# A hybrid attention trunk on one core: five buffers for the first modulation rows, two K tiles ahead of the weights, and c loaded as one row

## The chip, the core and the metric

The kernel runs on one core of a Trainium2 chip. A core has a matrix engine (TensorE: PE for its matmuls, PEld for its weight loads), three engines for elementwise work (VectorE: DVE, ScalarE: ACT, GpSimd: POOL), an engine that here only issues transfers (SyncE: SP), and 16 DMA engines that carry what SP's and ACT's queues hand them. Matmuls read SBUF and accumulate in PSUM banks. The metric is device microseconds (us) of one launch; lower is better.

## What is computed

A streaming encoder of two layers, batch 1, 256 tokens, model width 2048, all in float32. A conditioning vector `c` of 2048 numbers gives each layer six modulation vectors of 2048 (shift, scale and gate for the mixer, the same for the FFN):

```python
c_act = jax.nn.silu(c)
for i in range(DEPTH):
    mod = c_act @ ada_w[i] + ada_b[i]
    sh1, sc1, g1, sh2, sc2, g2 = [m[:, None, :] for m in jnp.split(mod, 6, axis=-1)]
    h = rms_norm(x, norm_mix_g[i]) * (1.0 + sc1) + sh1
    y = even_mixer(h, ...) if i % 2 == 0 else odd_mixer(h, ...)
    x = x + g1 * y
    h = rms_norm(x, norm_ffn_g[i]) * (1.0 + sc2) + sh2
    x = x + g2 * conv_ffn(h, ...)
return rms_norm(x, final_g)
```

The even mixer (layer 0) projects `h` once by `ev_w_in` (2048 columns in, 3400 out) to the queries, keys and values of sliding-window attention and of a sparse latent attention with an index; the odd mixer is stick-breaking attention. The FFN is gated with a short convolution over tokens, 5632 wide.

## The kernel before, in words

Activations lie feature-major: 16 K tiles (`DB`) of 128 features by 256 tokens. `xT` is the input in that form, loaded in four transfers. The kernel is written with a tile framework: pools hand out named tiles with a number of buffers for each tag, a new tile of a tag waits until the one whose buffer it takes has been read for the last time, and a scheduler places the instructions on each engine. Each engine, and SP's queue of transfers, then runs its list strictly in order.

**Weights.** All weight matrices stream through in pieces of 128 x 1024 (512 KiB). `make_piece` (L145 on) takes a tile `w` of tag `ring` (6 buffers) and has SP load it. Pieces of the first projection (`w_ev`) are multiplied as they are, in float32. For all later pieces ScalarE writes a rounded copy `hi` (L159) and VectorE the rest `lo` (L161), each in three buffers of a pool `split`, and TensorE runs three matmuls for one: hi x hi, hi x lo, lo x hi (`dense`, `pair_steps` L213 to L215, `token_steps`). `units` makes one piece ahead (`AHEAD`) of the one in use.

**Modulation.** The modulation is done as 192 jobs (`JOBS`), in the order in which they are used: scale and shift row of K tile 0, of K tile 1, and so on. `ada_step` (L107 on) takes a tile of tag `ada` (two buffers of 128 x 2048, 1 MiB), has SP load the job's weights (L118), and VectorE multiplies them by `c_act`, which holds silu(c) in every partition, and sums along the row (L120). For a scale row a short instruction (L124) makes the factor `a`. `ada_until` runs jobs up to the one that is needed; `beat`, called with each weight piece, spreads the later ones over the time.

**The opening** (`even_mixer`, L425 on). The sum of squares of `xT` is formed by ScalarE (L416) and VectorE (L420) in tiles `sq_in` of the pool `split`, TensorE sums over partitions (`nps_in`), GpSimd takes the power, and `r_in` is the reciprocal norm. Then a loop over the 16 K tiles: `modulate` runs the tile's two modulation jobs, VectorE writes `xn_m` = r x a x xT (L319), ScalarE adds the shift and writes `hT_m` (L321), and TensorE multiplies that tile into eight open PSUM accumulators (`c_lat`, `va` L221 and six `pair` L228: 16 matmuls, a step here), which takes two weight pieces. After the loop come the rest of the projections and the attention (`q` L234 is the first matmul there).

**The start.** SP loads `c_act` (c already repeated for 128 partitions, 1 MiB), then `xT`, then the early parameters `par`; ScalarE's queue loads small constants (`con` among them). ScalarE applies silu to all of `c_act` (L103).

## Time and profile before

| | |
|---|---|
| Time, median of 3 runs | 2358.72 us (2341.0 to 2361.32) |
| The profiled execution: time, span | 2362.08 us, 2360.3 us |
| TensorE matmuls busy | 2283.0 us (97% of the span) |
| VectorE, ScalarE, GpSimd busy | 1738.4, 1092.9, 12.0 us |
| Mean granted clock of TensorE | 0.99 |
| Moved by DMA | 606.03 MB, mean 257 GB/s |
| `ada` loads | 192 of 1024 KB |
| Weight loads `w` | 528 + 96 + 64 + 58 of 512 KB |

The span runs from the first to the last instruction of one profiled execution. A busy matmul engine is not an engine at its peak, since matmuls are pipelined and their ends are modelled. In a timeline a row gives the start, the time from the first instruction of the row to the end of its last, engine, source line, operation, what it writes and reads, and in brackets how long the engine was idle before and what ended that. The chain of waits goes back from the last instruction of a stretch to what released it each time. The granted clock is given as a share of TensorE's 2.4 GHz.

### The profile page before, as it was taken

The numbers are of one execution on the slowest core, as the hardware profiler recorded it, in microseconds if no ns is written. First come the engines' busy times: TensorE is split into PE (matmuls) and PEld (weight loads), VectorE is DVE, ScalarE is ACT, GpSimd is POOL, SyncE is SP. The second block draws the span as 40 slices with busy tenths as digits, with TensorE's granted clock in tenths as the row PEclk, the third lists the DMA queues.
The fourth block names the chain that finished last, engine by engine and source line by source line (L and its number), as shares of the span: only waits on it lengthen the run. The fifth ranks groups of instructions, "written<-read, shape, count | busy, mean of one in ns | idle before, by whom it ended". The sixth has DMA issues, their size and how long they took to land.

```text
span 2360.3 us, 44197 instructions
## 1 busy us (share of the span) xinstructions
PE 2283.0 (97%) x18340; PEld 2240.1 (95%) x18340; DVE 1738.4 (74%) x2390; ACT 1092.9 (46%) x1553; POOL 12.0 (1%) x26
## 2 busy tenths in 40 slices
PE   5889999899999999999999999999999999999998
PEld 4768899899999999999999999999999999999998
DVE  4557689998887888888887676878766656656655
ACT  1013354455553554454456655645555445445434
POOL 1000000000000000000000000000000000000000
PEclk9999999999999999999999999999999999999999
DMA  8998988788888888888867777676766666666663
GB/s 313 344 335 326 331 305 312 286 313 302 303 298 299 304 300 304 300 304 301 304 226 240 237 238 239 226 260 204 231 188 187 187 186 185 188 187 187 188 187 118
DMA packets 141929, 606.03 MB, mean 257 GB/s; under 512 B 15584, under 2 KB 20256, under 8 KB 117024
## 3 DMA queue, kind: packets, MB, share of 16 engines
q1 hardware_dynamic: 136656, 597.67, 74.8%
q10 hardware_dynamic: 5072, 5.54, 0.8%
q8 instruction: 143, 2.34, 0.4%
q14 instruction: 58, 0.48, 0.1%
HBM read 601.00 MB, written 2.15 MB: 256 GB/s over the span
## 4 chain that ended last, share of the span: by engine, by line
PE 53%; issue 32%; DMA 7%; DVE 6%; ACT 1%; POOL 0%; ACTq 0%; DVEq 0%; POOLq 0%; SPq 0%
PE up L215 7%; PE up L213 7%; PE up L214 7%; DMA ada<-in_w_ada_dram 6%; DVE ada L120 4%; PE dn L213 3%; PE dn L214 3%; PE dn L215 3%; PE o L213 2%; PE o L215 2%; PE o L214 2%; PE cq L213 1%; PE ck L213 1%; PE cq L214 1%; PE ck L214 1%
## 5 line engine op out<-in xcount | busy, mean ns | idle before, releaser
L159 ACT ACTIVATE hi<-w 128x1024 fp32r<-128x1024 f32 x688 | 728.6, 1059 | 890.7 <-PE up L214 389.6
L161 DVE TENSOR_TENSOR lo<-w,hi 128x1024 fp32r<-128x1024 f32 x688 | 840.5, 1223 | 402.5 <-ACT hi L159 399.9
L213 PE MATMUL up<-hT_f,hi 128*128 128x256 f32 x2816 | 789.5, 281 | 2.8 <-ACT hT_f L323 2.2
L215 PE MATMUL up<-hT_f,lo 128*128 128x256 f32 x2816 | 788.6, 280 | 0.2 <-DVE lo L161 0.2
L214 PE MATMUL up<-hT_f,hi 128*128 128x256 f32 x2816 | 787.4, 280 | 0.0
L213 PEld LDWEIGHTS up<-hT_f,hi 128*128 128x128 f32 x2816 | 529.5, 188 | 3.7 <-ACT hT_f L323 2.9
L215 PEld LDWEIGHTS up<-hT_f,lo 128*128 128x128 f32 x2816 | 530.6, 189 | 0.5 <-DVE lo L161 0.4
L214 PEld LDWEIGHTS up<-hT_f,hi 128*128 128x128 f32 x2816 | 529.9, 188 | 0.0
L120 DVE CUSTOM_DVE_ANT_0 ada<-ada,c_act,par 128x2048 f32<-128x2048 f32 x192 | 450.5, 2346 | 78.8 <-DMA ada<-in_w_ada_dram 78.7
L214 PE MATMUL dn<-gT,hi 128*128 128x256 f32 x1364 | 383.8, 281 | 0.0
L215 PE MATMUL dn<-gT,lo 128*128 128x256 f32 x1364 | 383.8, 281 | 0.0
L213 PE MATMUL dn<-gT,hi 128*128 128x256 f32 x1364 | 383.8, 281 | 0.0
L215 PEld LDWEIGHTS dn<-gT,lo 128*128 128x128 f32 x1364 | 262.1, 192 | 0.0
L213 PEld LDWEIGHTS dn<-gT,hi 128*128 128x128 f32 x1364 | 256.1, 188 | 0.0
L214 PEld LDWEIGHTS dn<-gT,hi 128*128 128x128 f32 x1364 | 256.1, 188 | 0.0
L228 PE MATMUL pair<-hT_m,w 128*128 128x256 f32 x384 | 89.1, 390 | 0.0
L228 PEld LDWEIGHTS pair<-hT_m,w 128*128 128x128 f32 x384 | 76.6, 199 | 11.6
L349 DVE SCALAR_TENSOR_TENSOR xT<-dn,mod,xT 128x256 f32<-128x256 f32 x128 | 56.4, 478 | 25.4 <-PE dn L215 20.2
L228 PE MATMUL q<-hT_m,w 128*128 128x256 f32 x320 | 73.7, 382 | 0.0
L213 PE MATMUL cq<-hT_m,hi 128*128 128x256 f32 x256 | 72.2, 282 | 1.1 <-ACT hT_m L323 1.1
L214 PE MATMUL cq<-hT_m,hi 128*128 128x256 f32 x256 | 72.1, 282 | 0.0
L213 PE MATMUL ck<-hT_m,hi 128*128 128x256 f32 x256 | 72.0, 281 | 0.0
(260 smaller groups left out, 3071.3 us busy)
## 6 DMA issues: line engine op xcount, KB each, us to landing
w<-in_w_f_dram SPq DMA_DIRECT2D x528, 512.0 KB, 4.4
ada<-in_w_ada_dram SPq DMA_DIRECT2D x192, 1024.0 KB, 6.5
w<-in_w_od_dram SPq DMA_DIRECT2D x96, 512.0 KB, 4.4
w<-in_w_o_dram SPq DMA_DIRECT2D x64, 512.0 KB, 5.3
w<-in_w_ev_dram SPq DMA_DIRECT2D x58, 512.0 KB, 7.9
bias<-bias_rows ACTq DMA_DIRECT2D x16, 256.0 KB, 6.2
xT<-in_x_dram SPq DMA_DIRECT2D x4, 512.0 KB, 7.6
c_act<-in_c_dram SPq DMA_DIRECT2D x1, 1024.0 KB, 4.9
```

The lines of the kernel that those rows point to most:

```text
L120: nc.vector.tensor_tensor_reduce(w, w, c_act, scale=1.0, scalar=pr("ada_b")[:, s * DB + b:s * DB + b + 1], op0=ALU.mult, op1=ALU.add, accu ...
L159: nc.scalar.activation(hi, raw, AF.Copy)
L161: sub = nc.vector.tensor_tensor(lo, raw, hi.bitcast(F32), op=ALU.subtract)
L213: nc.tensor.matmul(o, hi[:, js], xh, start=k == first and j == 0, stop=False, skip_group_check=True)
L214: nc.tensor.matmul(o, hi[:, js], xl, start=False, stop=False, skip_group_check=True)
L215: nc.tensor.matmul(o, lo[:, js], xh, start=False, stop=k == last, skip_group_check=True)
L228: nc.tensor.matmul(acc[:, j * S:(j + 1) * S], w[:, j * P:(j + 1) * P], xs[:, k], start=k == first and j == 0, stop=k == last, skip_group_c ...
L349: nc.vector.scalar_tensor_tensor(xT[:, b], acc, g, xT[:, b], op0=ALU.mult, op1=ALU.add)
```

## The change

Five things change. `c` is loaded as a single row of 2048 numbers (into a buffer of tag `ada`); four matmuls with a row of ones spread it over 128 partitions into four PSUM banks, and ScalarE applies silu from there, 512 columns at a time. Of the first 32 modulation jobs the odd ones (the shift rows of layer 0's mixer) take their buffer from the pool `split`, whose tiles are now 8 KiB a partition and there are three of them; the even ones (scale rows) keep the two `ada` buffers. For that, `hi` and `lo` of a weight piece become the two halves of one tile `parts`. The `sq_in` tiles move to tiles that the mixer uses later. In the opening the modulation jobs of K tile k + 2 (`LEAD`) are asked for before the work on K tile k.

```diff
--- before.py
+++ after.py
@@ -28,6 +28,7 @@
 PIECE = 8
 RING = 6
 AHEAD = 1
+LEAD = 2
 SH1, SC1, G1, SH2, SC2, G2 = range(6)
 
 JOBS = []
@@ -72,7 +73,8 @@
         return ps.tile([P, 512], F32, tag=tag, bufs=BANKS[tag], name=name)
 
     c_act = keep.tile([P, D], F32, name="c_act")
-    nc.sync.dma_start(c_act, c)
+    c_row = ring.tile([P, D], F32, tag="ada", bufs=2, name="c_row")[:1]
+    nc.sync.dma_start(c_row, c)
     par = keep.tile([P, P_W], F32, name="par")
     rb = keep.tile([32, 32], F32, name="rb")
     nc.scalar.dma_start(rb, rel_bias)
@@ -100,7 +102,12 @@
     nc.vector.memset(mhalf, -0.5)
 
 
-    nc.scalar.activation(c_act, c_act, AF.Silu)
+    one_row = keep.tile([1, P], F32, name="one_row")
+    nc.vector.memset(one_row, 1.0)
+    for i, tag in enumerate(("acc", "acc", "s", "s")):
+        spread = bank(tag, f"c_ps{i}")
+        nc.tensor.matmul(spread, one_row, c_row[:, i * 512:(i + 1) * 512], start=True, stop=True)
+        nc.scalar.activation(c_act[:, i * 512:(i + 1) * 512], spread, AF.Silu)
     mod = keep.tile([P, 12, DB], F32, name="mod")
     scaled = {(l, k): keep.tile([P, DB], F32, name=f"a_{k}{l}") for k in (SC1, SC2) for l in (0, 1)}
     pace = {"rate": 0.0, "due": 0.0, "hold": 0, "behind": False}
@@ -114,7 +121,10 @@
         ada["made"] += 1
         layer, kind, b = JOBS[i]
         s = layer * 6 + kind
-        w = ring.tile([P, D], F32, tag="ada", bufs=2, name=f"ada{i}")
+        if i < 2 * DB and i % 2:
+            w = split.tile([P, D], F32, tag="parts", name=f"ada{i}")
+        else:
+            w = ring.tile([P, D], F32, tag="ada", bufs=2, name=f"ada{i}")
         nc.sync.dma_start(w, w_ada[i])
         end = mod[:, s, b:b + 1]
         nc.vector.tensor_tensor_reduce(w, w, c_act, scale=1.0, scalar=pr("ada_b")[:, s * DB + b:s * DB + b + 1],
@@ -155,9 +165,9 @@
             flow["pieces"][i] = (raw,)
             beat()
             return
-        hi = split.tile([P, n], F32R, tag="hi", name=f"hi{i}")
+        parts = split.tile([P, 2, n], F32R, tag="parts", name=f"parts{i}")
+        hi, lo = parts[:, 0], parts[:, 1]
         nc.scalar.activation(hi, raw, AF.Copy)
-        lo = split.tile([P, n], F32R, tag="lo", name=f"lo{i}")
         sub = nc.vector.tensor_tensor(lo, raw, hi.bitcast(F32), op=ALU.subtract)
         flow["pieces"][i] = (hi, lo)
         if pace["behind"]:
@@ -412,7 +422,7 @@
             hT = keep.tile([P, DB, S], F32, tag="hT", name="hT_m0")
             total = None
             for k in range(0, DB, 4):
-                sq = split.tile([P, 4, S], F32, tag="lo", name=f"sq_in{k}")
+                sq = pool.tile([P, 4, S], F32, tag="oS1" if k == 0 else "oS2" if k % 8 else "qi", bufs=1, name=f"sq_in{k}")
                 nc.scalar.activation(sq, xT[:, k:k + 4], AF.Square)
                 if total is None:
                     total = sq
@@ -424,6 +434,7 @@
             early = [(token_steps32, bank("acc", "c_lat")), (token_steps32, bank("acc", "va"))]
             early += [(pair_steps32, bank(tag, f"pair{i}")) for i, tag in enumerate(("acc", "s", "s", "o", "t", "t"))]
             for k in range(DB):
+                ada_until(0, SH1, min(k + LEAD, DB - 1))
                 modulate(hT, r, 0, SC1, SH1, "m0", [k])
                 for steps_, acc in early:
                     if steps_ is token_steps32:
@@ -866,7 +877,7 @@
     out = {}
     out["x"] = f["x"][0].T.reshape(DB, P, S).transpose(1, 0, 2)
     sink_order = [8 * (g // 2) + 4 * (s // 2) + 2 * (g % 2) + s % 2 for g in range(4) for s in range(4)]
-    out["c"] = broadcast(f["c"])
+    out["c"] = f["c"].reshape(1, D)
     out["params"] = np.concatenate([
         cols(f["ada_b"], 2), cols(f["norm_mix_g"], 2), cols(f["norm_ffn_g"], 2), cols(f["final_g"], 1),
         broadcast(f["ev_sinks"][0][sink_order]), broadcast(f["ev_kv_norm_g"][0]), cols(f["ffn_conv_w"], 6),
```

The scheduler puts this into each engine's list. Below is SP's list of transfers right after `par`, first before the change (`ada_147` and `ada_151` are the scale and the shift row of K tile 0, `ada_179` and `ada_183` those of K tile 1, `w_157` the first weight piece):

```order
L118 DMA ada_147<-in_w_ada_dram 128x2048
L118 DMA ada_151<-in_w_ada_dram 128x2048
L152 DMA w_157<-in_w_ev_dram 128x1024
L152 DMA w_159<-in_w_ev_dram 128x1024
L152 DMA w_169<-in_w_ev_dram 128x1024
L118 DMA ada_179<-in_w_ada_dram 128x2048
L118 DMA ada_183<-in_w_ada_dram 128x2048
L152 DMA w_189<-in_w_ev_dram 128x1024
```

and the same place after the change (`ada_161` and `ada_165` are K tile 0, `ada_168` and `ada_172` K tile 1, `ada_175` and `ada_179` K tile 2, `ada_207` and `ada_211` K tile 3, `w_185` the first weight piece):

```order
L128 DMA ada_161<-in_w_ada_dram 128x2048
L128 DMA ada_165<-in_w_ada_dram 128x2048
L128 DMA ada_168<-in_w_ada_dram 128x2048
L128 DMA ada_172<-in_w_ada_dram 128x2048
L128 DMA ada_175<-in_w_ada_dram 128x2048
L128 DMA ada_179<-in_w_ada_dram 128x2048
L162 DMA w_185<-in_w_ev_dram 128x1024
L162 DMA w_187<-in_w_ev_dram 128x1024
L162 DMA w_197<-in_w_ev_dram 128x1024
L128 DMA ada_207<-in_w_ada_dram 128x2048
L128 DMA ada_211<-in_w_ada_dram 128x2048
L162 DMA w_217<-in_w_ev_dram 128x1024
```

Six modulation rows now stand ahead of the first weight piece, where two stood; from there on it is two rows and two pieces in turn, as before. After the last row six pieces follow where two did.

VectorE's list from the last addition of squares on, before the change (`ISA` with three inputs is a reduction, the `ISA` behind it reads its sum out):

```order
L420 TENSOR_TENSOR sq_in_110<-sq_in_110,sq_in_118 128x1024
L304 TENSOR_SCALAR v_in<-nps_in 128x2
L120 ISA ada_147,mod<-ada_147,c_act,par 128x2048
L120 ISA mod 128x1
L124 SCALAR_TENSOR_TENSOR a_93<-mod,par 128x1
L319 SCALAR_TENSOR_TENSOR xn_m_154<-r_in,a_93,xT 128x256
L120 ISA ada_151,mod<-ada_151,c_act,par 128x2048
```

and after it:

```order
L430 TENSOR_TENSOR sq_in_124<-sq_in_124,sq_in_132 128x1024
L130 ISA ada_161,mod<-ada_161,c_act,par 128x2048
L130 ISA mod 128x1
L314 TENSOR_SCALAR v_in<-nps_in 128x2
L134 SCALAR_TENSOR_TENSOR a_107<-mod,par 128x1
L130 ISA ada_165,mod<-ada_165,c_act,par 128x2048
```

The first reduction now stands ahead of the norm's `v_in`, and the first shift row's reduction ahead of the first `xn_m` (which follows it). Further on the scheduler has also placed some instructions of the mixer and the first FFN a little earlier or later among each other.

## Rows read from the trace of the kernel before

**Rows 1.** Windows: stretch, length; busy us (instructions) by engine; clock; DMA share; GB/s.
```profile
0.00:180.00 180.00, 133.06 (x544) 109.74 (x544) 91.00 (x111) 23.21 (x46) 7.82 (x20) 0.95 0.89 332
600.00:1000.00 400.00, 400.00 (x3398) 400.00 (x3397) 338.37 (x424) 188.32 (x240) 0.00 (x0) 1.00 0.87 302
```

**Rows 2.** Chain of waits, 0 to 200 us: start us, us, what.
```profile
25.29 5.12 DMA ada<-in_w_ada_dram
...
77.68 5.72 DMA ada<-in_w_ada_dram
...
136.55 7.62 DMA ada<-in_w_ada_dram
```

**Rows 3.** Waits, 0 to 180 us: us in total, times, longest us.
```profile
DVE ada L120 <- DMA ada<-in_w_ada_dram: 58.9, 17, 5.0
```

**Rows 4.** The waits of SP's own queue, 0 to 180 us, same columns.
```profile
SPq L118 <- DVE a L124: 76.7, 15, 9.6
```

**Rows 5.** Timeline, one round of the opening: start us, us, what [idle before <-releaser].
```profile
136.55 3.38 SPq L118 DMA_DIRECT2D ada<-in_w_ada_dram  x2
...
140.03 1.11 SPq L152 DMA_DIRECT2D w<-in_w_ev_dram  x2
...
140.18 1.13 PE L221 MATMUL c_lat<-w,hT_m 128*128 128x256 f32 x4 [2.92 <-ACT hT_m L321]
...
146.59 3.38 SPq L118 DMA_DIRECT2D ada<-in_w_ada_dram  x2
```

**Rows 6.** Timeline, TensorE: first, second and last step's start, next stage's first matmul.
```profile
30.36 2.08 PE L221 MATMUL c_lat<-w,hT_m 128*128 128x256 f32 x4 [3.81 <-ACT hT_m L321]
...
39.85 1.03 PE L221 MATMUL c_lat<-w,hT_m 128*128 128x256 f32 x4
...
170.63 1.13 PE L221 MATMUL c_lat<-w,hT_m 128*128 128x256 f32 x4 [1.15 <-ACT hT_m L321]
...
177.64 1.46 PE L234 MATMUL q<-hT_m,w 128*128 128x256 f32 x6
```

**Rows 7.** Windows: four stretches of the opening, columns as in rows 1.
```profile
8.00:20.00 12.00, 1.24 (x5) 0.78 (x4) 4.44 (x6) 7.09 (x6) 0.00 (x0) 1.00 1.02 417
60.00:90.00 30.00, 26.78 (x121) 22.32 (x120) 19.86 (x24) 2.03 (x4) 0.00 (x0) 1.00 0.99 376
90.00:160.00 70.00, 54.73 (x223) 45.04 (x221) 36.90 (x42) 3.05 (x6) 0.00 (x0) 0.93 0.87 310
166.00:180.00 14.00, 12.82 (x61) 10.64 (x59) 5.73 (x12) 8.12 (x24) 0.73 (x1) 1.00 1.02 408
```

**Rows 8.** Timeline of the first 28 us: what stands ahead of the first reduction.
```profile
7.01 1.46 PE L398 MATMUL vb_ps<-oh,rb 32*32 32x384 f32 x2 [7.01 <-DMA oh<-in_onehot_dram]
...
11.44 1.91 ACT L103 ACTIVATE c_act<-c_act 128x2048 f32<-128x2048 f32 x1
...
13.26 2.93 ACT L416 ACTIVATE sq_in<-xT 128x1024 f32<-128x1024 f32 x3
...
16.61 2.56 DVE L420 TENSOR_TENSOR sq_in<-sq_in,sq_in 128x1024 f32<-128x1024 f32 x2
...
22.91 2.34 DVE L120 CUSTOM_DVE_ANT_0 ada<-ada,c_act,par 128x2048 f32<-128x2048 f32 x1
...
27.01 0.48 DVE L319 SCALAR_TENSOR_TENSOR xn_m<-r_in,a,xT 128x256 f32<-128x256 f32 x1 [1.55 <-ACT r_in L423]
```

**Rows 9.** Waits from 180 us to the end: us in total, times, longest us.
```profile
ACT hi L159 <- PE up L214: 389.6, 284, 3.2
...
PE up L215 <- DVE lo L161: 0.2, 1, 0.2
```

**Rows 10.** Timeline in the first FFN: one weight piece split, and the next.
```profile
699.69 1.06 ACT L159 ACTIVATE hi<-w 128x1024 fp32r<-128x1024 f32 x1 [1.17 <-PE up L214]
...
700.78 1.23 DVE L161 TENSOR_TENSOR lo<-w,hi 128x1024 fp32r<-128x1024 f32 x1 [1.24 <-ACT hi L159]
...
702.52 1.06 ACT L159 ACTIVATE hi<-w 128x1024 fp32r<-128x1024 f32 x1 [1.32 <-issue]
```

## The prediction

> **What bounds the kernel now.** I read the busy times by stage first. TensorE is busy without a gap in a stretch of 400 us in the middle, but only 133.1 of the first 180 us [rows 1]. So time can be won at the front and nowhere near as easily behind it: what the opening loses, the rest, which is TensorE after TensorE, carries to the end unchanged. That is why I add what happens before 180 us to the end of the program one to one.
>
> Next comes the chain of waits inside the opening. It is one pattern, repeated for each of the 15 K tiles after the first: a load of a modulation row (`ada`) lands, VectorE reduces it in 2.35 us, the next load is issued, and that takes 5 to 8 us to land. The first such load takes 5.12 us (with no other transfer under way), one at 77.68 takes 5.72 us, one at 136.55 takes 7.62 us [rows 2]. VectorE stands idle for these loads 58.9 us in 17 waits [rows 3], and SP, which issues them, is itself blocked 76.7 us on the same reductions [rows 4]. One round is in [rows 5]: SP issues at 136.55 and next at 146.59, 10.04 us later; in between TensorE starts its step 2.92 us late. The cause is that the scale rows share two buffers with the shift rows: a load can't be issued before the row two places ahead of it is consumed. It is latency in a loop, not work: VectorE's own work per tile is two reductions of 2.35 us and three short instructions.
>
> What would the step cost otherwise? TensorE's 16 matmuls of a step take 7.01 us (from the last step's start, 170.63, to the first matmul of the next stage, 177.64), and 9.49 us in the first step, 30.36 to 39.85, which begins slower [rows 6]. A step's transfers are two `ada` rows of 1 MiB and two weight pieces of 0.5 MiB, 3.146 MB. In the two stretches in which requests are queued without a break, 8 to 20 and 166 to 180 us, the rate is 417 and 408 GB/s; in the opening's loop it is 376 (60 to 90 us) and then 310 (90 to 160 us) [rows 7]. At 408 GB/s a MiB takes 2.57 us and a step 7.71 us. So the transfers, no longer the loop, would set the pace, TensorE 10% behind them.
>
> **The change part by part.** *Buffers.* Scale rows now have the two `ada` buffers to themselves and shift rows three others. Before a scale row is issued, the row of two K tiles earlier must be reduced, no longer that of the tile just before. Between landing and use there are then some 5 MiB queued, 13 us at 408 GB/s, against 2.35 us for a reduction and at most another 3 us of VectorE's queue ahead of it. The loop's wait is covered, with room. The weight ring (6 pieces) asks that TensorE be done three steps back, which it is as long as TensorE is less than two steps late. So I take the steady pace from the transfers.
>
> *The start.* This part can lose. The first weights now stand behind six modulation rows in SP's queue, not two, and the third scale row (`ada_175`) waits for the reduction of the first. That reduction needs all of `c_act` and stands behind VectorE's last addition of squares, which ends at 16.61 + 2.56 = 19.17 [rows 8]. The reduction takes 2.34 us, and before the change SP issued its next load 0.04 us after it, at 25.29 [rows 2, 8]: 21.6 here. A lone load of 5.12 us [rows 2] then lands at 26.7; the shift row behind it 2.57 us; the first weight piece 1.29 us: 30.6. TensorE's first step began at 30.36 [rows 6], so the start is about where it was. The modulated tile is there by then: the first normalised tile starts at 27.01 [rows 8], and its shift row has already been reduced.
>
> *c as one row.* It takes 1 MiB off the queue (2.57 us at 408 GB/s) and lets the con and x tiles land sooner. Against that stand four matmuls of 512 columns and four activations in place of one of 1.91 us. A matmul of this kind is the first of the trace, 384 columns in 1.46 us, right after a long idle time [rows 8]; for 512 columns that is 1.95 us, four make 7.8 us after 8.47, so 16.3, and the last quarter of the activation (0.5 us) 16.8 where it ended at 13.35: 3.4 us late at worst, with the squares behind it. At best everything is 2.57 us earlier. The two are near each other in size, matmuls that follow each other get faster, so I take nothing, and keep -2.6 and +3.4 us for the range; both go to the end one to one, since the third scale row hangs on them.
>
> *hi and lo in one tile.* After the opening ScalarE may write `hi` of a new piece only when TensorE has done the last `lo` matmul of the piece three back, one matmul later than before (0.12 us: a piece is 24 matmuls and lasts 2.83 us, below). ScalarE does wait for just this release today, 389.6 us in the first kind of matmul alone; TensorE waits 0.2 us for `lo` there [rows 9]. The slack: `hi` starts at 699.69, `lo` is done at 700.78 + 1.23 = 702.01, 2.32 us after the release; the next piece's `hi` starts at 702.52, so a piece lasts 2.83 us, and two whole pieces, 5.66 us, lie between release and use [rows 10]. 3.3 us of cover swallow 0.12. Cost: nothing; without cover 688 pieces would pay 0.12 each, 83 us. The squares in other tiles, the memset and the order in which the scheduler puts later VectorE work are costed at nothing too: TensorE waits there for hardly anything [rows 9]; I keep 3 us either way.
>
> **The sum.** The last weight that can hold TensorE up is piece 27, behind the last modulation rows; from then on pieces follow each other at 1.29 us and TensorE is the slower. Between the first piece and piece 27 lie 26 rows and 27 pieces, 39.5 MiB, 101.5 us at 408 GB/s: 30.6 + 101.5 = 132.1. Half a step (3.5), then two whole steps (14.0): the opening ends at 149.6, where it ended at 177.6. That is 28.0 us less. The profiled execution took 2362.1 us (its span 2360.3 and 1.8 around it), 3.4 above the median of the three runs shown. 2362.1 - 28.0 = 2334.1. I don't take off the 3.4 us: the loop is what varies most here, and it is gone.
>
> The Trainium skill has a rule against this. "DMA: Bandwidth & Descriptors", section Bandwidth, says that between HBM and SBUF a core's share of HBM, about 358 GB/s, is what binds. By it a step would take 8.79 us and the kernel about 2349 us (an estimate from the page's figure); I give that 0.04, inside rival 1. The trace disagrees: 417 and 408 GB/s over 12 and 14 us [rows 7].
>
> **Rivals.**
> 1. *The rate sinks.* 12 and 14 us at over 400 GB/s are short, and most of 120 us is asked for here. If it stays at the 376 GB/s of 60 to 90 us, a MiB takes 2.79 us: first piece at 30.9, piece 27 at 141.1, end 158.6, 19.0 us saved: 2343. For it: in those 30 us the transfer engines count as 99% busy. Against it: the queue ran dry in each round there, which the busy share may hide.
> 2. *The slow phase is no loop.* From 90 us on a round takes 10 us and the rate is 310 GB/s. If that comes from one slow transfer engine and not from the loop, a deeper queue doesn't help: 3.38 us a MiB, piece 27 at 165.4, end 182.9: 5.3 us more than before, 2367. Break-even is 322 GB/s. Against it: from 166 to 180 us, right behind that phase, the rate is 408.
> 3. *hi and lo.* Slower by up to 83 us if the chain release, `hi`, `lo`, use were tight; it decides once 3.3 us of slack a piece are gone, and pays for more than the gain from 0.04 us a piece on. With the gain taken off, at most 2417. Rows 9 and 10 speak against it; only where VectorE is nearly full (180 to 600 us) may it pay a little.
> 4. *The transfers are faster still.* Then TensorE alone sets the opening: 30.6 + 9.49 + 15 x 7.01 = 145.2, 32.4 us saved, 2330; with an early c 2327.
>
> **How the numbers follow.** Rates of 395 to 420 GB/s and a start within 2 us of 30.6, thus 2328 to 2339: 0.63, forecast 2334. Rival 1, 2339 to 2350: 0.20. Rival 2: 0.07. Rival 3: 0.03. Rival 4, under 2328: 0.07. The range 2327 to 2347 leaves out rivals 2 and 3, the upper end of rival 1 (0.05) and the lower end of rival 4 (0.03): 0.18. A measurement of this kernel can tell about 1% from no change: under 2335.1 against the median of 2358.7. The forecast stands right at that line: 0.38 of the first case's 0.63 and all of rival 4 lie below it, together 0.45; slower by over 1% needs rival 3, 0.03; within 1% is the rest, 0.52.
>
> **What would show it.** VectorE's idle time for `ada` loads in the opening goes from 58.9 us to under 20, most of it waits of two us a step for landing data, with loads landing 13 us or more after issue; SP's wait on VectorE at the third scale row from about 14 to 21.6. First weights multiply at 29 to 32 us, the next stage's first matmul comes at 147 to 153, the rate from 35 to 130 us is over 395 GB/s, and TensorE's idle time before `c_lat` nearly vanishes. From there to the end the span is 2182.7 us as before, within 3. Wrong would be: 310 to 376 GB/s with requests queued (rivals 1, 2), or TensorE waiting for `lo` or `hi` after the opening (rival 3).

## The result, and the profile of the changed kernel

The changed kernel takes 2321.68 us (median of 4 runs, 2320.58 to 2337.73), the kernel before 2357.97 us (4 runs, 2341.0 to 2361.32) beside it: a ratio of 0.9884, 95% interval [0.9849, 0.9919] (the ratio on record is an estimate over the runs; the two medians alone give 0.9846). Two later comparisons of the same two programs gave 0.9865 [0.9831, 0.9900] and 0.9895 [0.9861, 0.9930]. The profiled execution's span is 2320.7 us, 39.6 less than before. Of these, 28.5 went in the opening, as forecast. The other 11 were not forecast. Part of them is a pace of TensorE that the old program shows too, as the runs below tell; that the change has no hand in the rest is not shown.

The windows of the changed kernel, columns as in [rows 1]; what answers to [rows 7] is 60 to 138 us, and the last two lines answer to [rows 1]:

```profile
20.00:31.00 11.00, 4.26 (x18) 3.77 (x18) 7.83 (x10) 0.89 (x2) 2.81 (x1) 1.00 0.72 276
31.00:60.00 29.00, 28.57 (x120) 24.76 (x121) 23.75 (x28) 2.54 (x5) 0.00 (x0) 1.00 1.02 419
60.00:90.00 30.00, 29.65 (x137) 25.55 (x137) 21.10 (x24) 2.03 (x4) 0.00 (x0) 1.00 1.02 417
90.00:138.00 48.00, 45.90 (x207) 38.51 (x206) 31.66 (x36) 3.04 (x6) 0.00 (x0) 1.00 1.02 415
...
0.00:150.00 150.00, 128.95 (x545) 105.81 (x546) 93.01 (x114) 22.27 (x45) 7.97 (x20) 1.00 0.97 389
600.00:1000.00 400.00, 400.00 (x3399) 400.00 (x3398) 340.75 (x424) 191.47 (x239) 0.00 (x0) 1.00 0.87 301
```

Look at the last column: 310 to 376 GB/s had become 415 to 419, over 107 us without a break. TensorE is busy 128.95 us of the first 150, where it had been 133.1 of 180.

The chain of waits in the opening (start us, us, what), which had been load, reduction, load [rows 2]:

```profile
39.22 2.26 DVE ada L130
42.41 13.99 DMA w<-in_w_ev_dram
...
101.69 14.97 DMA w<-in_w_ev_dram
...
116.72 14.98 DMA w<-in_w_ev_dram
131.70 0.04 issue
131.75 3.72 PE pair L238 x16
```

From 42.4 us on no reduction stands in it. (Ahead of that, from 28.7 to 41.5 us, it holds five reductions of 2.26 us, nearly back to back; the 39.22 line is the last of them.) One weight load follows another, each 15 us from issue to landing, since a deep queue lies ahead of it: at 415 GB/s, 15 us are 6.2 MB, the transfers of two steps of 7.5 us. The waits up to 149.1 us (us in total, times, longest), VectorE's and SP's, against [rows 3, 4]:

```profile
DVE ada L130 <- DMA ada<-in_w_ada_dram: 23.8, 11, 2.8
...
SPq L128 <- DVE a L134: 38.1, 13, 6.0
...
SPq L128 <- DVE mod L130: 7.8, 1, 7.8
SPq L128 <- PE c_ps L109: 6.6, 1, 6.6
```

The second of SP's lines is the third scale row's wait for the first reduction. The last is a wait that the change brought along: the row of `c` lies in one of the two buffers of the scale rows, so the second scale row is issued only when the matmuls that spread `c` have read it.

And the timeline of the same kernel (start us, us, engine, line), first step, last step and what follows, against [rows 6, 8] (the profile records each float32 matmul of a step twice, so x24 is 12 matmuls):

```profile
17.75 2.56 DVE L430 TENSOR_TENSOR sq_in<-sq_in,sq_in 128x1024 f32<-128x1024 f32 x2
20.23 2.35 DVE L130 CUSTOM_DVE_ANT_0 ada<-ada,c_act,par 128x2048 f32<-128x2048 f32 x1
23.45 1.09 SPq L162 DMA_DIRECT2D w<-in_w_ev_dram  x2
31.43 2.05 PE L231 MATMUL c_lat<-w,hT_m 128*128 128x256 f32 x4 [3.67 <-DMA w<-in_w_ev_dram]
41.04 1.03 PE L231 MATMUL c_lat<-w,hT_m 128*128 128x256 f32 x4
...
143.94 5.34 PE L238 MATMUL pair<-hT_m,w 128*128 128x256 f32 x24
149.12 1.46 PE L244 MATMUL q<-hT_m,w 128*128 128x256 f32 x6
```

The opening ends at 149.12 us, where the next stage's first matmul starts; it had ended at 177.64.

For the rest of the document the program is cut at TensorE's first start in each stage: the opening up to the first `q`; the first mixer; the 2112 `up` matmuls that open the first feed-forward stage; the rest of that stage; the second feed-forward stage, from the norm ahead of it to the end. (The second mixer, left out, took 398.6 to 399.9 us in every profile.) All in us, from one profile each:

| kernel | first weights | opening ends | first mixer | first 2112 `up` | rest of 1st feed-forward | 2nd feed-forward | span |
|---|---|---|---|---|---|---|---|
| before | 30.4 | 177.6 | 270.0 | 251.9 | 497.5 | 764.0 | 2360.3 |
| before, second profile | 30.6 | 170.0 | 269.1 | 252.9 | 488.1 | 754.4 | 2333.3 |
| changed | 31.4 | 149.1 | 267.6 | 256.8 | 497.5 | 750.0 | 2320.7 |
| changed, second | 31.5 | 148.9 | 267.8 | 254.1 | 488.1 | 755.8 | 2313.8 |
| changed, third | 31.4 | 149.0 | 270.4 | 254.2 | 488.1 | 755.8 | 2317.0 |
| before + c as one row | 29.3 | 170.7 | 270.2 | 252.3 | 497.5 | 755.0 | 2344.8 |
| before + lead | 30.6 | 181.6 | 269.2 | 252.3 | 488.1 | 755.2 | 2345.0 |
| before + hi, lo in one tile | 30.6 | 176.2 | 271.8 | 256.8 | 497.5 | 764.7 | 2366.8 |
| changed, no lead | 29.4 | 146.6 | 270.1 | 255.0 | 488.1 | 749.8 | 2309.5 |
| changed, c broadcast | 34.6 | 152.5 | 264.7 | 256.9 | 497.5 | 755.6 | 2327.0 |
| spare tiles, no lead | 29.2 | 147.7 | 272.4 | 244.8 | 490.5 | 754.0 | 2308.8 |
| spare tiles, lead from step 2 | 29.2 | 142.7 | 272.4 | 252.6 | 497.5 | 763.3 | 2328.0 |
| the same, second | 29.2 | 142.8 | 271.6 | 252.7 | 497.5 | 763.1 | 2327.1 |

From before to changed (first profiles): -28.5 in the opening, -2.4 in the first mixer, +4.9 in the first `up` block, 0.0 behind it, +0.4 in the second mixer, -14.0 in the second feed-forward stage: -39.6.

### The profile page after: what moved, and what is told of

It is laid out like the page before. It is cut to its first block, busy times and chain, and to the rows that moved or that the text cites. A ratio compares the mean times of both kernels' runs of the same rounds, so it can differ in the third digit from the quotient of the medians.

```text
span 2320.7 us, 44174 instructions
## 1 busy us (share of the span) xinstructions
PE 2268.5 (98%) x18348; PEld 2225.5 (96%) x18348; DVE 1739.4 (75%) x2391; ACT 1106.3 (48%) x1556; POOL 12.2 (1%) x26
## 4 chain that ended last, share of the span: by engine, by line
PE 54%; issue 33%; DMA 6%; DVE 4%; ACT 1%; POOL 0%; SPq 0%; DVEq 0%; POOLq 0%; ACTq 0%
PE up L225 7%; PE up L223 7%; PE up L224 7%; DMA w<-in_w_ev_dram 4%; PE dn L223 3%; PE dn L225 3%; PE dn L224 3%; DVE ada L130 2%; PE o L223 2%; PE o L225 2%; DMA ada<-in_w_ada_dram 2%; PE o L224 2%; PE q L238 1%; PE cq L223 1%; PE ck L223 1%
## 5 line engine op out<-in xcount | busy, mean ns | idle before, releaser
L171 DVE TENSOR_TENSOR parts<-w,parts 128x1024 fp32r<-128x1024 f32 x688 | 840.0, 1222 | 332.0 <-ACT parts L170 331.1
L170 ACT ACTIVATE parts<-w 128x1024 fp32r<-128x1024 f32 x688 | 728.0, 1059 | 705.6 <-PE up L225 253.1
L223 PE MATMUL up<-hT_f,parts 128*128 128x256 f32 x2816 | 787.7, 280 | 3.9 <-ACT hT_f L333 2.2
L225 PE MATMUL up<-hT_f,parts 128*128 128x256 f32 x2816 | 786.6, 280 | 1.3 <-DVE parts L171 1.3
L224 PE MATMUL up<-hT_f,parts 128*128 128x256 f32 x2816 | 787.2, 280 | 0.0
L223 PEld LDWEIGHTS up<-hT_f,parts 128*128 128x128 f32 x2816 | 531.5, 189 | 5.0 <-ACT hT_f L333 2.9
L225 PEld LDWEIGHTS up<-hT_f,parts 128*128 128x128 f32 x2816 | 530.9, 189 | 2.2 <-DVE parts L171 2.2
L224 PEld LDWEIGHTS up<-hT_f,parts 128*128 128x128 f32 x2816 | 531.3, 189 | 0.0
L130 DVE CUSTOM_DVE_ANT_0 ada<-ada,c_act,par 128x2048 f32<-128x2048 f32 x192 | 450.1, 2346 | 41.5 <-DMA ada<-in_w_ada_dram 41.4
L224 PE MATMUL dn<-gT,parts 128*128 128x256 f32 x1364 | 380.8, 279 | 0.0
L225 PE MATMUL dn<-gT,parts 128*128 128x256 f32 x1364 | 380.8, 279 | 0.0
L223 PE MATMUL dn<-gT,parts 128*128 128x256 f32 x1364 | 380.7, 279 | 0.0
L225 PEld LDWEIGHTS dn<-gT,parts 128*128 128x128 f32 x1364 | 258.9, 190 | 0.0
L223 PEld LDWEIGHTS dn<-gT,parts 128*128 128x128 f32 x1364 | 256.8, 188 | 0.0
L224 PEld LDWEIGHTS dn<-gT,parts 128*128 128x128 f32 x1364 | 256.0, 188 | 0.0
L781 ACT ACTIVATE ug<-up,par 128x256 f32<-128x256 f32 x88 | 49.7, 565 | 140.9 <-PE up L225 140.9
L782 DVE SCALAR_TENSOR_TENSOR ug<-up,par,ug 128x255 f32<-128x255 f32 x88 | 42.4, 482 | 60.0 <-ACT ug L781 59.6
L223 PE MATMUL cq<-hT_m,parts 128*128 128x256 f32 x256 | 72.2, 282 | 1.1 <-ACT hT_m L333 1.1
L224 PE MATMUL cq<-hT_m,parts 128*128 128x256 f32 x256 | 72.1, 281 | 0.0
```

The source lines that it names most:

```text
L130: nc.vector.tensor_tensor_reduce(w, w, c_act, scale=1.0, scalar=pr("ada_b")[:, s * DB + b:s * DB + b + 1], op0=ALU.mult, op1=ALU.add, accu ...
L170: nc.scalar.activation(hi, raw, AF.Copy)
L171: sub = nc.vector.tensor_tensor(lo, raw, hi.bitcast(F32), op=ALU.subtract)
L223: nc.tensor.matmul(o, hi[:, js], xh, start=k == first and j == 0, stop=False, skip_group_check=True)
L224: nc.tensor.matmul(o, hi[:, js], xl, start=False, stop=False, skip_group_check=True)
L225: nc.tensor.matmul(o, lo[:, js], xh, start=False, stop=k == last, skip_group_check=True)
```

## Experiments

### The two programs once more: where the other 11 us are from

Of the change, the second feed-forward stage has only the shared tile for hi and lo, and TensorE waits for next to nothing there in either profile. Yet the last `dn` block goes faster. A hundred microseconds in it, before and changed (columns as in [rows 1]; the first bracket counts TensorE's matmuls):

```profile
2230.00:2330.00 100.00, 100.00 (x852) 100.00 (x851) 56.76 (x67) 43.81 (x50) 0.00 (x0) 1.00 0.61 183
```

```profile
2195.00:2295.00 100.00, 100.00 (x884) 100.00 (x884) 58.81 (x69) 45.31 (x53) 0.00 (x0) 1.00 0.62 185
```

852 matmuls against 884 in the same time (the count takes in those that a window's edge cuts), with TensorE never idle and the granted clock 1.00 in both. From start to start, over the whole block, a matmul takes 117.8 ns before and 113.3 ns after. Is this the change? Both programs were profiled again without an edit.

> The changed kernel once more, for its scatter. The opening, which waits for transfers alone, should repeat: first weights multiply at 31 to 32 us, the next stage begins at 148 to 151 us. If TensorE's two cadences come and go by themselves, the feed-forward stages differ from the first profile in which blocks run at 113.3 ns a matmul, in whole blocks, and times scatter over 17 to 35 us. If the cadence belongs to this kernel, the same blocks run at 113.3 ns and times stay within a few us of 2321.

> The kernel before, profiled a second time, as a control. If the two cadences of TensorE belong to the run and not to the program, whole feed-forward blocks run at 113.3 ns a matmul here too, other ones than in the first profile. If the opening's loop of landing, reduction and issue has no fixed length, its rounds differ from the first profile's (8 to 10 us) and it ends somewhere between 168 and 184 us instead of at 177.6.

The kernel before, second profile, the same block:

```profile
2205.00:2305.00 100.00, 100.00 (x885) 100.00 (x884) 59.32 (x71) 46.46 (x54) 0.00 (x0) 1.00 0.63 188
```

So the old program does it too: TensorE has two cadences in these stages, and which one a `dn` block gets belongs to the run. In all thirteen profiles a cadence changed only at the border of two blocks, or at a wait in the first `up` block of a stage, never inside an unbroken stretch. In the table, "rest of 1st feed-forward" is 497.5 us where all its blocks run slowly and 488.1 where its 2112 `dn` matmuls run fast: 9.4 us, 4.45 ns a matmul. The three profiles of the changed kernel differ among themselves in the same way: the first has slow `dn` blocks in the first stage and the fast cadence in most of the second's first `up` block, the other two have all `dn` blocks fast and no `up` block.

This accounts for one part of the 14.0 us that the second feed-forward stage lost between the first profiles, and not for the other. Some 7.8 us lie behind its first `up` block, where `dn` ran fast, as in the old program. But 6.2 lie in the first `up` block itself (250.1 and 244.0 us), and a first `up` block in the fast cadence was seen in three of the eight profiles with buffers of their own for the shift rows (changed, changed without lead, spare tiles without lead) and in none of the five without. That is too few to say whether the change has a hand in it.

The two cadences are of the size of the scatter that is left: 16 runs of the changed kernel lie from 2315.6 to 2340.0 us (median 2325.1, mean 2327.5), 57 of the kernel before from 2330.1 to 2365.5 (mean 2352.8). The means are 25.3 us apart.

The openings tell the two programs apart better than the times do. The changed one's ends at 149.12, 148.9 and 149.0 us in three profiles, a chain of transfers that repeats to 0.2 us. The old loop's rounds differ from run to run (7.3 to 10.0 us in the second profile, without the regular 10 us late in the first): 177.6, then 170.0.

### The lead alone

```
             for k in range(DB):
+                ada_until(0, SH1, min(k + 2, DB - 1))
                 modulate(hT, r, 0, SC1, SH1, "m0", [k])
```

> The kernel before with the lead of two K tiles alone: scale and shift rows still share two buffers, c is broadcast by its load. Theory A (a row waits for the reduction two rows back, and that is the loop): the lead gives nothing, rounds of 8 to 10 us, the start a few us later since the first weights stand behind six rows of which four wait for reductions (first weights multiply at 33 to 40 us), the opening ends at 177 to 188 us, the time is 2358 to 2372 us. Theory B (the order of rows and weights is what counts): the opening ends before 160 us, the time is under 2342 us.

Measured: 2352.66 us, ratio 1.0019 [0.9987, 1.0050], no change. The opening ends at 181.6, 4 us later than in the first profile of before, as theory A has it; the first weights came sooner than it said (30.6), and the time is under its 2358; the profiled execution (2346.8) had fast `dn` blocks in both feed-forward stages. Its chain of waits:

```profile
41.21 6.93 DMA ada<-in_w_ada_dram
48.15 0.03 issue
48.17 2.35 DVE ada L120
...
50.56 7.04 DMA ada<-in_w_ada_dram
57.60 0.02 issue
57.63 2.35 DVE ada L120
...
60.02 8.36 DMA ada<-in_w_ada_dram
```

The loop is whole. SP is told to run two tiles ahead, and can't, since the row it wants to issue has no buffer. Order without buffers gave nothing here.

### Buffers without the lead

```
-LEAD = 2
+LEAD = 0
```

> The changed kernel without its lead: five buffers, but the rows of a K tile are issued right ahead of that tile's weights. Theory A (buffers alone break the loop; SP already runs ahead as far as the six weight pieces let it, three steps, 21 us, against 13 us of queue): rate over 400 GB/s from 35 to 130 us, weights of the first step no longer stand behind the third scale row, first weights multiply at 28 to 30 us, the opening ends at 143 to 149 us, the time is 2316 to 2334 us, no worse than the changed kernel. Theory B (the lead is what counts): rounds of 8 us and more come back, the opening ends after 157 us, the time is 2330 us or more.

Measured: 2333.04 us median of 10 runs (2311.06 to 2343.54), ratio 0.9923 [0.9887, 0.9959], and an opening that ends at 146.6, 2.5 us before the changed kernel's. Theory A, but for its rate before 60 us. First weights at 29.4: they no longer stand behind the third scale row. The other side of it, windows of 30 to 90 us:

```profile
30.00:60.00 30.00, 30.00 (x134) 26.20 (x133) 22.26 (x28) 2.03 (x4) 0.00 (x0) 1.00 0.88 345
60.00:90.00 30.00, 29.82 (x138) 25.93 (x137) 20.32 (x22) 2.03 (x4) 0.00 (x0) 1.00 1.02 417
```

and SP's waits up to 146 us:

```profile
SPq L162 <- PE pair L238: 80.8, 29, 10.7
```

SP now waits for TensorE to free weight pieces, and rows behind them in its queue wait along, so the transfer engines rest early on (345 GB/s), and from some 80 us on TensorE's steps take 7.5 us, as in the changed kernel. The two halves of the edit thus pull against each other: the buffers (with c as one row) win all of the 28 us, the lead fills the rate early on but puts six rows ahead of the first weights. In the time the 2.5 us don't show: the changed kernel's three ratios, 0.9865 to 0.9895, are if anything lower, with intervals that overlap.

### c as one row, alone and taken back

```
-    nc.sync.dma_start(c_act, c)
+    c_row = ring.tile([P, D], F32, tag="ada", bufs=2, name="c_row")[:1]
+    nc.sync.dma_start(c_row, c)
...
-    nc.scalar.activation(c_act, c_act, AF.Silu)
...
+        nc.tensor.matmul(spread, one_row, c_row[:, i * 512:(i + 1) * 512], start=True, stop=True)
+        nc.scalar.activation(c_act[:, i * 512:(i + 1) * 512], spread, AF.Silu)
```

> The kernel before with one part of the change: c loaded as one row and spread by TensorE. Theory (the row is worth nothing): silu ends about 1.1 us later, as after the change (14.5 us against 13.35), the loop between row loads and reductions stays, rounds late in the opening take 8 to 10 us, the next stage's first matmul comes at 177 to 181 us, the time is 2356 to 2363 us. Rival (the megabyte that c no longer loads is what brings the rate up): the opening ends before 165 us and the time is under 2350 us.

> The changed kernel with c broadcast by its load again (1 MiB more in the queue, silu as one activation). Theory (the row is worth what it takes off the queue, as the opening now waits for transfers from about 76 us on): 2.5 us more of transfers against a silu that ends about a us sooner: the opening ends at 148 to 152 us. Rival (the third scale row waits for the first reduction anyway, so the megabyte is hidden): it ends within 1 us of 149.1 or sooner. The time is within 5 us of the changed kernel's either way.

Alone it changes nothing that can be measured: 2347.02 us, ratio 1.0006 [0.9973, 1.0039]. That is under the rival's 2350, but so nearly was the kernel before beside it (2350.93). Its opening ended at 170.7, neither as theory nor as rival had it; the second profile of before ended at 170.0, so the loop's own scatter is enough to explain this. Taken out of the changed kernel, the opening ends at 152.5, 3.4 us later, just outside the expected range. The megabyte isn't the whole of it. VectorE's timeline there:

```profile
16.91 2.55 DVE L423 TENSOR_TENSOR sq_in<-sq_in,sq_in 128x1024 f32<-128x1024 f32 x2
23.13 0.16 DVE L307 TENSOR_SCALAR v_in<-nps_in 128x2 f32<-128x2 f32 x1 [3.67 <-PE nps_in L304]
23.21 2.34 DVE L123 CUSTOM_DVE_ANT_0 ada<-ada,c_act,par 128x2048 f32<-128x2048 f32 x1
```

The additions end at 19.5 us, 0.8 sooner than in the changed kernel, but then the first reduction stands behind `v_in`, which waits 3.67 us for TensorE, and starts at 23.21 instead of 20.23. The third scale row hangs on it, the first weights on that row (34.6 against 31.4). So most of what the row gave the changed kernel is that, with it, the scheduler put the reduction ahead of `v_in`. By the first feed-forward stage the 3.4 us are gone again in this profile: 417.2 us (152.5 + 264.7) against 416.7 to 419.4. The time, 2335.11 us (5 runs, ratio 0.9908 [0.9871, 0.9944]), is 12.9 above the changed kernel's beside it (2322.23), not within the 5 that were expected, though the intervals of the two ratios overlap. Of the 13.2 us between the two profiled spans, 9.4 are slow `dn` blocks in the first stage.

### hi and lo in one tile, alone

```
-        hi = split.tile([P, n], F32R, tag="hi", name=f"hi{i}")
+        parts = split.tile([P, 2, n], F32R, tag="parts", name=f"parts{i}")
+        hi, lo = parts[:, 0], parts[:, 1]
         nc.scalar.activation(hi, raw, AF.Copy)
-        lo = split.tile([P, n], F32R, tag="lo", name=f"lo{i}")
```

(The `sq_in` tiles move too, as in the change.)

> The kernel before with hi and lo in one tile of three buffers and the squares elsewhere, nothing else. Theory A (this costs nothing): the opening ends at 176 to 179 us, and the first 448 matmuls of the first feed-forward stage take 56 us as before. Rival (this part costs the changed kernel the 4.9 us that it lost there): they take 59 to 62 us. On matmul cadence: in the profile of the changed kernel 480 us ran at 113.3 ns a matmul in place of 117.8. If one tile for hi and lo is what brings that cadence, some 300 us or more run so here and the time is 2340 to 2350 us; if it comes and goes by itself, runs of this kernel and of the kernel before scatter between about 2341 and 2361 us alike.

Measured: 2362.16 us, ratio 1.0051 [1.0022, 1.0081]: slower, if by little. The rival: the first 448 matmuls take 60.8 us (55.9 before), and the first `up` block takes 256.8 us as in the first profile of the changed kernel, 4.9 more than before. The first mixer (+1.8), the second (+0.5) and the second feed-forward stage (+0.7) add a little; the 12 us that the ratio makes are not all found in the one profile. On the cadence this profile says no: none of its `up` blocks and none of its `dn` blocks ran fast. (The 480 us at 113.3 ns of the expectation are some 380 in the trace of the changed kernel: from 1614 to 1816 us, from 2004 to 2064, and from 2188 to the last `dn`.) ScalarE's timeline some 30 us into that block, before:

```profile
478.73 1.06 ACT L159 ACTIVATE hi<-w 128x1024 fp32r<-128x1024 f32 x1 [1.72 <-PE up L214]
479.70 0.55 ACT L770 ACTIVATE ug<-up,par 128x256 f32<-128x256 f32 x1
481.56 1.06 ACT L159 ACTIVATE hi<-w 128x1024 fp32r<-128x1024 f32 x1 [1.31 <-PE up L214]
482.64 1.28 ACT L781 ACT_TABLE_LOAD   x1
483.93 0.42 ACT L781 ACTIVATE ug<-ug 128x256 f32<-128x256 f32 x1
```

and with one tile, where it shows in TensorE's waits too:

```profile
480.44 1.06 ACT L160 ACTIVATE parts<-w 128x1024 fp32r<-128x1024 f32 x1 [1.76 <-PE up L215]
481.41 0.55 ACT L770 ACTIVATE ug<-up,par 128x256 f32<-128x256 f32 x1
483.27 0.56 ACT L770 ACTIVATE ug<-up,par 128x256 f32<-128x256 f32 x1 [1.32 <-PE up L215]
483.85 1.28 ACT L781 ACT_TABLE_LOAD   x1
...
486.68 2.00 ACT L160 ACTIVATE parts<-w 128x1024 fp32r<-128x1024 f32 x2
...
493.41 0.39 PE L213 MATMUL up<-hT_f,parts 128*128 128x256 f32 x1 [0.96 <-ACT parts L160]
```

Not the 0.12 us of the shared release costs, but an order. Before, ScalarE splits the next piece 2.8 us after the last and only then loads a table. With one tile the scheduler put a gated activation, the table load and four more ahead of the next `hi`, which comes after 6.2 us, two at once; some 5 us later TensorE waits for a split piece, and the granted clock is 0.93 over the 15 us around that wait. The windows, before and with one tile:

```profile
482.00:497.00 15.00, 15.00 (x129) 15.00 (x129) 14.35 (x23) 11.37 (x18) 0.00 (x0) 1.00 0.83 280
```

```profile
482.00:497.00 15.00, 13.18 (x99) 12.56 (x98) 13.51 (x23) 9.32 (x15) 0.00 (x0) 0.93 0.70 241
```

Thirty matmuls fewer in 15 us are some 3.5 of the 4.9 us; the rest lies ahead of it, in the opening of the block.

### A version meant to keep the gain and drop the costs

The opening's shift rows can lie where `kB` and `vB` lie later; hi and lo then keep their tiles, and `sq_in` its own. The main lines:

```
+        if i < 2 * DB and i % 2:
+            w = shift["pool"].tile([P, D], F32, tag=("kB", "vB")[i // 2 % 2], bufs=1, name=f"ada{i}")
+        else:
+            w = ring.tile([P, D], F32, tag="ada", bufs=2, name=f"ada{i}")
...
+                if k:
+                    ada_until(0, SH1, min(k + 1, DB - 1))
```

(the last two lines only in the second version, with c as one row in both)

> A version meant to be better: c as one row, hi and lo in tiles of their own as before the change, the opening's shift rows in the two tiles of 8 KB a partition that hold kB and vB later, no lead. Theory A (the loop needs own buffers only; one tile for hi and lo costs 4 to 5 us at the start of the first feed-forward stage, since the scheduler writes hi behind four other activations there): first weights at 29 to 30 us, opening ends at 145 to 149 us, the 2112 matmuls that open the first feed-forward stage take 252 us as before (255 to 257 in the changed kernel), and the time, cadence for cadence, is 5 to 8 us under the changed kernel's. Theory B (the stall there comes from something else in the change, for instance the earlier opening): they take 255 to 257 us here too.

> The same with a lead of one K tile from the second step on, so that the first weights still stand right behind the first two rows. Theory A (the transfer engines, 345 GB/s from 30 to 60 us without a lead since SP waits for a free weight piece, now run without a break, so that TensorE waits less at the end): rate over 400 GB/s from 30 to 140 us, opening ends at 141 to 145 us, 2 to 5 us under the version without a lead. Theory B (TensorE's own 7 us a step or the third scale row's wait uses this up): 145 to 149 us.

> The changed kernel a third time, beside the better version on the same chip: opening ends at 148 to 151 us; between 2310 and 2340 us by the cadence.

> The version with shift rows in the tiles of kB and vB and a lead of one from the second step on, again: opening ends at 142 to 144 us. Theory A (its gain over the changed kernel is the 6 us of the opening, as the 4 us won at the first feed-forward stage were lost in the mixer ahead of it): 3 to 8 us under the changed kernel in the mean. Theory B (no gain that reaches the end): within 2 us.

Windows of the second version, second profile:

```profile
30.00:60.00 30.00, 30.00 (x131) 26.07 (x131) 24.68 (x30) 2.54 (x5) 0.00 (x0) 1.00 1.01 412
60.00:90.00 30.00, 30.00 (x141) 26.41 (x140) 21.09 (x24) 2.03 (x4) 0.00 (x0) 1.00 1.02 416
90.00:138.00 48.00, 47.54 (x221) 41.53 (x220) 31.65 (x36) 4.05 (x9) 0.00 (x0) 1.00 1.02 415
```

TensorE is all but full from 30 us on, and transfers run above 410 GB/s beside it. Steps take 6.9 us nearly to the end, which comes at 142.7 and 142.8: theory A to the letter for the opening, 6.3 us before the changed kernel's. The first `up` block is back at 252.6 us (244.8 in the version without a lead, where most of it ran in the fast cadence; its first 448 matmuls, ahead of that, took 56.2 us, as before the change). So theory A holds for the cost of hi and lo in one tile, too. But the first mixer ahead of it takes 272 instead of 268 to 270, so the 4 us stay a wash; what makes the mixer longer was not found. And the end doesn't show the 6 us: 2327.15 (0.9872 [0.9843, 0.9901]) and 2328.82 us (0.9876 [0.9843, 0.9909]), medians of 6 runs each, beside the changed kernel's 2322.23 and 2333.78. In the mean that is 1.5 us more than the changed kernel beside it the first time and 4.3 less the second (theory A had 3 to 8 less). Both profiles of this version have every feed-forward block in the slow cadence, and of its 12 runs ten lie within 2326.4 to 2331.6, two at 2317.6 and 2318.3, lower by about one stage's fast `dn` blocks (9.4). The version without a lead: 2323.06 us, 0.9864 [0.9828, 0.9899]. So neither is shown to beat the changed kernel. What the second won in the opening stands in its profiles, and so does the slow cadence in every block, which I can't steer.

## Why the prediction was right, and where it wasn't

**The loop and its end: right.** Forecast 149.6 us for the end of the opening, measured 149.12, 148.9 and 149.0. The lead without buffers left the loop whole, the buffers without the lead broke it. Loads in the opening land 12.6 us (rows) and 14.0 us (weights) after issue by the median, forecast was 13 or more; VectorE's wait for rows fell from 58.9 to 23.8 us, a little over the 20 named. TensorE waited only once ahead of `c_lat`, 3.7 us for the first weights; in the steps after it waited 2.5 us for weights ahead of `pair`, in seven waits. The loop's wait is covered, as forecast, only from 42 us on; ahead of that SP's next rows still hung on VectorE's reductions.

**The rate: right, 2% low.** 408 GB/s taken, 415 to 419 measured. Transfers set the pace from 76 us on, 7.5 us a step where I had 7.71; up to there TensorE's own 6.91 us did. The sum holds all the same, since it counts the bytes up to piece 27: 132.1 us forecast, and the last load in the chain landed at 131.70. Rivals 1 and 2 are out: 376 and 310 GB/s were the loop's doing. By the figure of about 358 GB/s (the Trainium skill, "DMA: Bandwidth & Descriptors", section Bandwidth) a step would have taken 8.79 us, an estimate; the measurement decides against it here, 107 us at 415 and more on one core. The Trainium skill's "HBM Reference", section Specifications, says itself that a core streaming alone measures about 425, which the trace comes near. I should have weighed that sentence with the other.

**The start: right within 0.8 us, from two misses.** First weights at 31.43 (30.6 forecast). The additions of squares ended at 20.31, not 19.17, since spreading c puts silu's end 1.1 us later: I had taken nothing there, with 3.4 as the bound. SP's wait for the first reduction ended near 22.6 us, 1.0 later than worked out. That this reduction stands ahead of `v_in` on VectorE, and that 3 us hang on it, the prediction's sum took for granted without saying so. It did not have SP's 6.6 us at the second scale row either, which the wait for the first reduction hid.

**hi and lo for nothing: wrong.** They cost 1 to 5 us in the first `up` block (254.1 to 256.9 against 251.9 and 252.9). The step that failed is the one that priced the edit by the 0.12 us of its release in a steady stretch [rows 10]. The release was covered as worked out; the price was that another allocation made the scheduler write another order where VectorE is nearly full. Rival 3 had named the place, not the mechanism.

**"From there to the end as before, within 3": wrong by 11.1.** It was 2171.6 us, not 2182.7. Mixers and `up` block together made +2.9; the second feed-forward stage made -14.0, by the cadence (6.2 in its first `up` block, 7.8 behind it), which TensorE's busy share in [rows 1] couldn't show, since it is 100% in both.

**The sum, then.** 2334.0 was forecast, in a range of 2327 to 2347. The measured median, 2321.68, is 12.3 us under the forecast and 5.3 under the range; the second comparison's (2322.23) is under the range as well, the third's (2333.78) inside. The ratio of 0.9884 on the 2358.72 us shown makes 2331.4, and over all runs the means are 25.3 us apart, where 28.0 was forecast. That these come near is in part luck. I took the 28 us off one execution that lay near the top of the old kernel's scatter, its loop long and nearly all its blocks slow, and said that with the loop gone, what varies most was gone. The loop is gone; the larger part of the scatter stayed, and the cadence is of its size. The old opening lasted 170.0 to 177.6 us, so the gain that the change itself brings in the opening is 21 to 28.5 us, minus 1 to 5 for hi and lo. "Faster by over 1%" came out where I had given 0.45 to it and 0.52 to within 1%; with the forecast on the line, either was to be had.

**Rival 4** came true in another kernel, by its end and not by its condition: transfers were no faster there (412 to 416 GB/s), but asked for without a break from early on and with the first weights ahead of the lead. Then 29.2 us for the start and TensorE's own steps, 9.9 + 15 x 6.91, make 142.8, and the version with a late lead ends its opening at 142.7.

## What to carry to other kernels

A load that waits for the reduction of the load before it is a latency loop. Here more buffers broke it, and going further ahead in the order without them gave nothing. With them, a lead that stood ahead of the first weights cost the opening 2.5 us (149.1 against 146.6), and one that began behind them won 5.0 (142.7 against 147.7). Before a row of buffers is made out of another pool's tiles, look for tiles that are idle at that time, and price a changed allocation by the order that comes out of it, not by the release that it delays. Where a kernel's runs scatter by more than the change is worth, cut two profiles of each version into stages and compare stage by stage before explaining a difference in the total.

## What was not expected of the hardware

TensorE ran the same stream of 128x128 weights and 256 moving columns at 117.8 or at 113.3 ns a matmul, at a granted clock of 1.00 and without a wait. Per run, whole blocks of 520 to 1800 matmuls took the one or the other: `dn` blocks often the fast one, a stage's first `up` block three times in 26, its later `up` blocks never; the version whose two profiles were slow in all blocks had the narrowest scatter. A stage's `dn` blocks make 9.4 us of difference, a first `up` block 1790 x 4.45 ns = 8. No profile has both in full, since behind a fast first `up` block the first `dn` block was slow; between the sums of the three feed-forward columns in the table the versions with spare tiles lie 24 us apart (1489.3 and 1513.4). The Trainium skill, "TensorE: Matmul & The Clock Gate", section Back-to-back issue gap, gives 262 cycles for 256 columns, some 109 ns, for a matmul by itself; it says that in a stream of weight loads and matmuls both set the spacing, and has measured values for 128 and 512 columns (some 81 and 131 ns), none for 256. The two values here lie between those. What chooses between them was not found: a change came where a block begins or at a wait in a stage's first `up` block, but the same places stand in the other profiles without it, and none of the edits turned it on or off for certain.

One core drew 415 to 419 GB/s for 107 us in the changed kernel, and 412 to 416 for 108 us in the version with spare tiles and a late lead, beside a TensorE that was busy all but without a gap. In the loop, the same transfers ran at 310 to 376.
